# A bidirectional encoder layer on one core: row work between the layer's parts moved from GpSimd to VectorE, other tile order at the MLP's start, load order and held-back steps of the down products

## The chip, the core and the metric

One core of a Trainium2 chip. The time is the device time of one execution in microseconds (us); before is the median of three runs, beside one execution that was profiled. Engines are named as in the profile: PE (TensorE), ACT (ScalarE), DVE (VectorE), POOL (GpSimd), SP (SyncE, which issues the DMAs here).

## The reference, cut

```python
def trunk(x, ...):                       # x: prompt 256 tokens, sample 1024 tokens, D = 1024
    h = rms_norm(x, g_pre_mix)
    m = mixer(h, ...)                    # attention and retention branches, ends with merged @ w_out
    x = x + rms_norm(m, g_post_mix)
    h = rms_norm(x, g_pre_mlp)
    u = square(relu(h @ w_up))           # w_up 1024 x 4096
    return x + rms_norm(u @ w_down, g_post_mlp)   # w_down 4096 x 1024
```

Everything is float32. The prompt and the sample run through the same weights.

## The kernel before, in words

The 1280 tokens are ten row tiles of 128: tiles 0 and 1 are the prompt, 2 to 9 the sample. Each float32 product is made of three reduced-precision ones: `split` (L55) makes a high part on ACT (L57) and a low part on DVE (L58), and `mm3` (L60) issues high by high, high by low, low by high (L63 to L65). The kernel is written for a scheduler that orders each engine's instructions by a model of their times and by data dependences; pools of tiles add dependences when their space is used again.

**Seam 1**, at the end of `phase_merge`. `mm(t, u, w)` (L958) makes a quarter of w_out's product for row tile t in 24 matmuls of 256 columns, squares it on ACT with a running sum, and multiplies it by the gain on DVE (L965). `norm(t0)` (L967) does two row tiles: a reciprocal root on DVE (`rstd`, L67 to L80, 11 small instructions), the scaled add to x (for tiles 0 to 5 on ACT, L978, and POOL, L979; for tiles 6 to 9 one fused instruction on DVE, L975), a square sum on ACT (L981), a second root, and the scaling to the MLP's input (L985). `trow` (L996) transposes 128 x 512 of it on PE (four transposes, one bank) and splits the bank. The MLP's products are done by a scheme of seven products with sums and differences of blocks: the sums of row tiles (L1035, four for each of four pairs; those of i = 0 and 1 on POOL, those of 2 and 3 on DVE) are transposed into T[0] to T[2] and X[2] (from `tx` and from `mp`), the plain tiles into X[0] (prompt) and X[1]. The prompt's tiles come last in the w_out product, and its transposes last of all.

**The up phase** (`up(i)`, L1167, i = 0 to 15) runs seven products p1 to p7 and two plain ones for the prompt (c1, c2); `up_raw` loads the weights and `fprep` prepares their block sums (POOL) and splits. The results are squared and written to HBM as u rows (`u_s`, L1246).

**The down phase** (L1248 on) runs seven products over i = 0 to 15, in the order 1, 2, 6, 7, 4, 5, 3. `dprep(p, i)` loads a u row (`ur`, three buffers, L1264), in products 1 and 2 two weight tiles (`wd`, L1260), and splits both; `step` issues 15 matmuls for the five banks. `product(..., last)` holds the last steps back, so that each bank's matmuls of those steps come together. `part` squares half a row tile on ACT (L1319) and multiplies it by the gain on POOL (L1321); `final` has ten small DVE instructions and the scaled add of x (tiles 0 to 4: first half on ACT, L1340, and POOL, L1341, second half on DVE, L1343).

Of the kernel before, what the change touches and what calls it, by code (L numbers as in the profile page):

```python
# [35 lines left out]
FORD0 = ("A11", "A12", "S2", "S3", "S1", "A21", "A22", "S4")  # L36
# [12 lines left out]
class Build:  # L49
# [10 lines left out]
    def mm3(self, out, lhs, rhs, start, stop, more=False):  # L60
        (lh, ll), (rh, rl) = lhs, rhs
        mm = self.nc.tensor.matmul
        mm(out, lhsT=lh, rhs=rh, start=start, stop=False, skip_group_check=more)  # L63
        mm(out, lhsT=lh, rhs=rl, start=False, stop=False, skip_group_check=more)  # L64
        mm(out, lhsT=ll, rhs=rh, start=False, stop=stop, skip_group_check=more)  # L65
# [795 lines left out]
    def phase_merge(self):  # L861
# [105 lines left out]
        def norm(t0):  # L967
            ss = self.small.tile([P, 2], F32, tag="ss2", name="ss2")
            nc.vector.tensor_reduce(ss, ssa[:, t0:t0 + 2], AX.X, ALU.add)
            r = self.rstd(self.small, ss, D, 2)  # L970
            sx = self.small.tile([P, 2], F32, tag="sx2", name="sx2")
            for i in range(2):
                t = t0 + i
# [35 lines left out]
        for t in range(2, 6):  # L1009
            load_x(t)  # L1010
        self.up_raw(0)
        for t in range(2, 6):
            mm(t, 2, wo[2])
        self.fprep(0)
        self.fprep(1)
# [8 lines left out]
        for t in range(2, 6):  # L1024
            for h in range(2):
                trow(ms_[t][:, h * 512:(h + 1) * 512], X[1], 4 * h, (t - 2) * P)
        for u in (2, 3):
            for t in range(2):
                mm(t, u, wo[u])
        a_, b_ = slice(0, 512), slice(512, D)  # L1030
        t2s = []
        for i in range(4):
            xa, xb = ms_[2 + i], ms_[6 + i]
            e = nc.gpsimd if i < 2 else nc.vector
            sub = lambda o, x, y: e.tensor_tensor(o, x, y, ALU.subtract)  # L1035
            t2s.append(self.uw.tile([P, 512], F32, tag="t2", name="t2", bufs=3))
            sub(xa[:, a_], xb[:, a_], xa[:, a_])
            sub(t2s[i], xb[:, b_], xa[:, a_])
            sub(xb[:, a_], xb[:, b_], xb[:, a_])
            sub(xa[:, b_], xa[:, b_], t2s[i])  # L1040
        norm(0)
        self.close("mx", "w8r", "w8")
        tx = self.open("tx", 1)
        T = [(tx.tile([P, 4, 512], F32R, name=f"t{i}h"), tx.tile([P, 4, 512], F32R, name=f"t{i}l"))
             for i in range(3)]
        xtile(2)
        for j in range(5):
            for i in range(4):
                xa, xb = ms_[2 + i], ms_[6 + i]
                s, d, k = ((t2s[i], T[0], 0), (xb[:, a_], T[1], 0), (xa[:, a_], X[2], 0),  # L1050
                           (xa[:, b_], T[2], 0), (xb[:, b_], X[2], 4))[j]
                trow(s, d, k, i * P)
        for t in range(2):
            for h in range(2):
                trow(ms_[t][:, h * 512:(h + 1) * 512], X[0], 4 * h, t * P)
        self.X, self.T = X, T
        self.ul = self.open("ul", 1)
        self.sraw = [self.ul.tile([P, 4, P], F32, name=f"sr{i}") for i in range(4)]

    def up_raw(self, i):  # L1060
# [10 lines left out]

    def fprep(self, n):
# [7 lines left out]
        tt = nc.gpsimd.tensor_tensor  # L1080
        if f in ("A11", "A12", "A21", "A22"):
            src = {"A11": A11, "A12": A12, "A21": A21, "A22": A22}[f]
        else:
            s1, s2, s3, s4 = self.sraw
            if f == "S2":
                tt(s1, A21, A22, ALU.add)
                tt(s2, s1, A11, ALU.subtract)
            elif f == "S3":
                tt(s3, A11, A21, ALU.subtract)
            elif f == "S4":  # L1090
                tt(s4, A12, s2, ALU.subtract)
            src = {"S1": s1, "S2": s2, "S3": s3, "S4": s4}[f]
        if self.nfac % 6 < 3:
            p, tg = self.uw, "fe"
        else:
            p, tg = self.ul, "fl"
        self.nfac += 1
        hi = p.tile([P, 4, P], F32R, tag=tg + "h", name=tg + "h", bufs=3)
# [348 lines left out]
```

## Time and profile before

| | us |
|---|---|
| median of three runs (lowest, highest) | 2219.25 (2215.68, 2220.7) |
| the profiled execution's own time | 2216.62 |
| its span, first to last instruction | 2214.8 |
| PE busy in the span | 2078.1 (94%) |
| DVE busy | 1371.0 (62%) |
| ACT busy | 944.2 (43%) |
| POOL busy | 789.9 (36%) |

The profiled execution lies 1.8 us above its own span and 2.63 below the median. The up phase runs from about 1389 to 1790, the down phase from there to 2195.6, both with PE busy nearly all the time. What an engine waited for is read from rows that name the instruction that released it.

### The profile page before, as it was taken

To read this page: it belongs to the slowest core of one execution; us is meant where nothing else is said; L and a number is where in the kernel's file an instruction comes from. 1 tells how busy PE (TensorE), PEld (TensorE's weight loads), DVE (VectorE), ACT (ScalarE), POOL (GpSimd) and SP (SyncE) were. 2 spreads that over 40 slices of the span, in tenths; PEclk is the share of its full clock that TensorE was granted. 3 is DMA by queue.
4 is the path that set the end of the run, shared out by engine and by line. 5 is a ranking of instruction groups with operands and counts; after the bars stand their busy time and mean duration, and the time that the engine had idled before them with its cause. 6 is when DMAs were issued, how large, how long until landed. Compare 5 with 4: busy or idle time off the path is not lost. (4 is left out here: it accounts for less than half of the span.)

```text
span 2214.8 us, 32535 instructions
## 1 busy us (share of the span) xinstructions
PE 2078.1 (94%) x11856; PEld 1803.3 (81%) x11856; DVE 1371.0 (62%) x2754; ACT 944.2 (43%) x1912; POOL 789.9 (36%) x598
## 2 busy tenths in 40 slices
PE   7899999999988889898999995999999997999996
PEld 7788888888877778777888995888888875888885
DVE  7734645555599899987424429555555536754566
ACT  6422222222356666655423434444444433433442
POOL 1212111111056666665134524344444309720112
PEclk8999999999999999999999997999999999999998
DMA  3351111110322222221644512244333376333543
GB/s 146 120 187 39 43 41 41 41 41 25 104 58 83 71 84 84 75 64 58 221 161 131 167 48 105 86 141 148 135 123 128 136 272 235 99 100 96 164 139 113
DMA packets 169568, 241.09 MB, mean 109 GB/s; under 512 B 15768, under 2 KB 104768, under 8 KB 169408
## 3 DMA queue, kind: packets, MB, share of 16 engines
q1 hardware_dynamic: 161408, 230.82, 31.9%
q10 hardware_dynamic: 8000, 8.20, 1.1%
q8 instruction: 93, 1.52, 0.3%
q14 instruction: 67, 0.55, 0.1%
HBM read 159.91 MB, written 79.05 MB: 108 GB/s over the span
## 5 line engine op out<-in xcount | busy, mean ns | idle before, releaser
L63 PE MATMUL ps<-wh,uh 128*128 128x512 f32 x560 | 218.0, 395 | 17.2 <-ACT uh L57 12.2
L64 PE MATMUL ps<-wl,uh 128*128 128x512 f32 x560 | 219.9, 393 | 1.2 <-DVE wl L58 1.2
L65 PE MATMUL ps<-wh,ul 128*128 128x512 f32 x560 | 214.7, 390 | 0.0
L58 DVE TENSOR_TENSOR ul<-ur,uh 128x640 fp32r<-128x640 f32 x112 | 110.6, 990 | 144.4 <-ACT uh L57 144.4
L57 ACT CAST uh<-ur 128x640 fp32r<-128x640 f32 x112 | 81.8, 731 | 211.3 <-PE ps L64 177.5
L748 POOL TENSOR_TENSOR t<-s 128x1024 f32<-128x1024 f32 (+1 forms) x40 | 92.0, 2299 | 167.9 <-ACT s L742 109.9
L711 DVE TENSOR_REDUCE mx<-s 128x256 f32<-128x2048 f32 (+1 forms) x40 | 130.5, 3263 | 23.6 <-ACT s L706 23.4
L63 PE MATMUL ps<-hTh,wgh 128*128 128x512 f32 (+1 forms) x384 | 141.4, 368 | 2.4 <-ACT s L706 1.6
L63 PEld LDWEIGHTS ps<-wh,uh 128*128 128x128 f32 x560 | 106.5, 190 | 41.5 <-ACT uh L57 14.0
L64 PE MATMUL ps<-hTl,wgh 128*128 128x512 f32 (+1 forms) x384 | 138.3, 360 | 0.0
L65 PE MATMUL ps<-hTh,wgl 128*128 128x512 f32 (+1 forms) x384 | 138.3, 360 | 0.0
L63 PE MATMUL ps<-wah,hTh 128*128 128x512 f32 x320 | 127.9, 400 | 0.0
L64 PEld LDWEIGHTS ps<-wl,uh 128*128 128x128 f32 x560 | 106.4, 190 | 24.2 <-DVE wl L58 2.0
L65 PE MATMUL ps<-wah,hTl 128*128 128x512 f32 x320 | 125.0, 391 | 0.0
L64 PE MATMUL ps<-wal,hTh 128*128 128x512 f32 x320 | 124.7, 390 | 0.0
L65 PEld LDWEIGHTS ps<-wh,ul 128*128 128x128 f32 x560 | 105.7, 189 | 22.0
L58 POOL TENSOR_TENSOR el<-s,eh 128x1024 fp32r<-128x1024 f32 (+1 forms) x40 | 95.0, 2375 | 67.3 <-ACT eh L57 67.3
L507 POOL TENSOR_TENSOR qk<-t,t 128x256 f32<-128x256 f32 x40 | 29.4, 736 | 241.1 <-DVE t L503 194.0
L58 DVE TENSOR_TENSOR wl<-wd,wh 128x512 fp32r<-128x512 f32 x112 | 102.4, 914 | 20.5 <-ACT wh L57 20.5
L1177 POOL TENSOR_TENSOR a<-a 128x640 f32<-128x640 f32 x64 | 85.9, 1353 | 75.6 <-ACT a L1200 59.3
L500 DVE TENSOR_TENSOR t<-ps,rcs 128x256 f32<-128x256 f32 x40 | 17.0, 424 | 154.2 <-ACT v L494 136.8
L1321 POOL TENSOR_TENSOR acc<-acc,g 128x512 f32<-128x512 f32 x20 | 29.2, 1487 | 211.7 <-ACT jk L1319 211.7
(339 smaller groups left out, 6770.4 us busy)
## 6 DMA issues: line engine op xcount, KB each, us to landing
u_s<-a SPq DMA_DIRECT2D x112, 320.0 KB
ur<-u_s SPq DMA_DIRECT2D x112, 320.0 KB
uraw<-w_up SPq DMA_DIRECT2D x32, 512.0 KB
wd<-w_down SPq DMA_DIRECT2D x64, 256.0 KB
wraw<-w_in SPq DMA_DIRECT2D x24, 512.0 KB
x<-xs SPq DMA_DIRECT2D x16, 512.0 KB
g_s<-g SPq DMA_DIRECT2D x32, 256.0 KB
sg<-g_s SPq DMA_DIRECT2D x32, 256.0 KB
```

The costliest lines, as they stand in the source:

```text
L57: nc.scalar.copy(hi, src)
L58: (eng or nc.vector).tensor_tensor(lo, src, hi.bitcast(F32), ALU.subtract)
L63: mm(out, lhsT=lh, rhs=rh, start=start, stop=False, skip_group_check=more)
L64: mm(out, lhsT=lh, rhs=rl, start=False, stop=False, skip_group_check=more)
L65: mm(out, lhsT=ll, rhs=rh, start=False, stop=stop, skip_group_check=more)
L500: nc.vector.tensor_tensor(t0, pv, bc(rcs[:, pt, 0]), ALU.mult)
L507: nc.gpsimd.tensor_tensor(qk[:, 0:4].rearrange("p (j b) d -> p j b d", j=2), dup(t0[:, 0:2]), dup(t1[:, 0:2]), ALU.add)
L711: nc.vector.tensor_reduce(mx, s[:, 0:u[2]].rearrange("p k q -> p q k"), AX.X, ALU.max)
L748: nc.gpsimd.tensor_tensor(t[:, 0:n], src[:, 0:n], src[:, n:2 * n], ALU.add)
L1177: nc.gpsimd.tensor_tensor(r[:, s], r[:, s], r[:, s], ALU.mult)
L1321: nc.gpsimd.tensor_tensor(acc[t][:, c], acc[t][:, c], g3[:, c], ALU.mult)
```

## The change

It has four parts.

- **Norms and sums on DVE.** `norm` takes any row tiles and makes the scaled add of all of them with the fused DVE instruction; all the row sums are DVE's. The block sums of the first weights (`fsums`, on POOL) are made early, S3 and S4 in place.
- **Order at seam 1.** All row tiles but 7, 8, 9 get their third quarter first; norms go in the order 0/1, 2/3, 4/5, 6/7, 8, 9. The steps p1, p2, c1, c2 of `up(0)` come before the sums are transposed (`tprep`, called inside `up(0)`). T[0] and T[1] now lie in X[2], and T[2] to T[4] (T4, T1, B22) in `tx`.
- **Down loads.** In `dprep`, the two weight loads of products 1 and 2 are queued behind their own u row (`issue_after` adds an order on the issuing engine, no wait). In product 6 one block subtraction is made a product earlier.
- **The end.** Six steps of product 3 are held back instead of four, two of them in buffers of `wd`; `step` keeps the tiles in order; the gain of the last half row tiles and both halves of `final` are DVE's.

```diff
-        def norm(t0):
+        def norm(*ts):
+            t0, nt = ts[0], len(ts)
...
-                if t0 >= 6:
-                    nc.vector.scalar_tensor_tensor(xs[t], ms_[t], r[:, i:i + 1], xs[t], ALU.mult,
-                                                   ALU.add)
-                else:
-                    nc.scalar.activation(ms_[t], ms_[t], AF.Copy, scale=r[:, i:i + 1])
-                    nc.gpsimd.tensor_tensor(xs[t], xs[t], ms_[t], ALU.add)
+                nc.vector.scalar_tensor_tensor(xs[t], ms_[t], r[:, i:i + 1], xs[t], ALU.mult,
+                                               ALU.add)
...
-        for t0, t2 in ((2, (6, 7)), (4, (8,)), (6, (9,)), (8, ())):
+        for t0, t2 in ((0, 6), (2, 7), (4, 8)):
             for t in (t0, t0 + 1):
                 mm(t, 3, wo[3])
-            norm(t0)
-            for t in t2:
-                mm(t, 2, wo[2])
+            norm(t0, t0 + 1)
+            mm(t2, 2, wo[2])
         xtile(0)
         xtile(1)
...
+        nat(0, 1)
+        mm(6, 3, wo[3])
+        mm(7, 3, wo[3])
+        norm(6, 7)
+        mm(9, 2, wo[2])
+        nat(2, 3)
+        mm(8, 3, wo[3])
+        norm(8)
+        mm(9, 3, wo[3])
+        norm(9)
+        nat(4, 5)
...
-            e = nc.gpsimd if i < 2 else nc.vector
-            sub = lambda o, x, y: e.tensor_tensor(o, x, y, ALU.subtract)
...
+        def tprep():
+            sub = lambda o, x, y: nc.vector.tensor_tensor(o, x, y, ALU.subtract)
...
+            T = [(X[2][0][:, 0:4], X[2][1][:, 0:4]), (X[2][0][:, 4:8], X[2][1][:, 4:8])]
...
+            T += [(tx.tile([P, 4, 512], F32R, name=f"t{i}h"),
+                   tx.tile([P, 4, 512], F32R, name=f"t{i}l")) for i in range(3)]
...
+            if i == 0:
+                s_p1()
+                s_p2()
+                s_c1()
+                s_c2()
+                for n in range(4, 7):
+                    self.fprep(n)
+                self.tprep()
...
-                order = ((s_p1, 0), (s_p2, 1), (s_p6, 2), (s_p7, 3), (s_c1, 3), (s_p5, 4),
-                         (s_c2, 6), (s_p4, 6), (s_p3, 7))
+                order = ((s_p6, 4), (s_p7, 5), (s_p4, 6), (s_p5, 6), (s_p3, 7))
...
-        def dprep(p, i):
+        def dprep(p, i, wide=False):
             uraw = us.tile([P, HB], F32, tag="ur", name="ur", bufs=3)
-            nc.sync.dma_start(out=uraw, in_=self.u_s[UIDX[p], i])
-            for j, h in {1: ((0, 0), (1, 0)), 2: ((1, 1), (0, 1))}.get(p, ()):
-                load_wd(i, j, h)
+            ld = nc.sync.dma_start(out=uraw, in_=self.u_s[UIDX[p], i])
+            with self.tc.issue_after(ld.ins):
+                for j, h in {1: ((0, 0), (1, 0)), 2: ((1, 1), (0, 1))}.get(p, ()):
+                    load_wd(i, j, h)
...
+                with self.tc.issue_after(end.ins) if end and len(fs) > 1 else nullcontext():
+                    for n, (uh, ul, wh, wl) in enumerate(fs):
+                        end = self.mm3(bs[j], (uh[:, s], ul[:, s]), (wh, wl), start and n == 0,
+                                       stop and n == len(fs) - 1, more)
...
-            nc.gpsimd.tensor_tensor(acc[t][:, c], acc[t][:, c], g3[:, c], ALU.mult)
+            e = nc.vector if t < 5 and c is hi_ else nc.gpsimd
+            e.tensor_tensor(acc[t][:, c], acc[t][:, c], g3[:, c], ALU.mult)
...
-                if t < 5 and c is lo_:
-                    nc.scalar.activation(y, y, AF.Copy, scale=r)
-                    nc.gpsimd.tensor_tensor(y, y, x[:, c], ALU.add)
-                else:
-                    nc.vector.scalar_tensor_tensor(y, y, r, x[:, c], ALU.mult, ALU.add)
+                nc.vector.scalar_tensor_tensor(y, y, r, x[:, c], ALU.mult, ALU.add)
...
-        product(3, bc, False, 4)
-        for j in range(6):
-            if j < 5:
-                add(q1[j][:, hi_], q1[j][:, hi_], bc[j])
-                part(j, hi_)
-            if j:
-                final(j - 1)
+        product(3, bc, False, 6)
+        for j in range(5):
+            add(q1[j][:, hi_], q1[j][:, hi_], bc[j])
+            part(j, hi_)
+            final(j)
```

PE at the seam, before: `t_` are row sums (t2), `m_13099` and `m_13100` the rows of the sample, `m_13098` those of the prompt; `w8h` is w_out, `feh` the first up weight.

```order
L65 MATMUL ps<-w8h,mTl_12573 128x256
L999 MATMUL ps<-ident,t_14481 128x128 x4
L999 MATMUL ps<-ident,t_14486 128x128 x4
L999 MATMUL ps<-ident,t_14491 128x128 x4
L999 MATMUL ps<-ident,t_14496 128x128 x4
L999 MATMUL ps<-ident,m_13100 128x128 x16
L999 MATMUL ps<-ident,m_13099 128x128 x32
L999 MATMUL ps<-ident,m_13100 128x128 x16
L999 MATMUL ps<-ident,m_13098 128x128 x16
L63 MATMUL ps<-h2h_14315,feh 128x512
L64 MATMUL ps<-h2l_14316,feh 128x512
L65 MATMUL ps<-h2h_14315,fel 128x512
```

PE at the same place of the changed kernel; the first row is the last one of the steps p1, p2, c1, c2, and `h2h_14684` is X[2], that is T[0], with which p6 begins.

```order
L65 MATMUL ps<-h2h_14255,fel 128x512
L994 MATMUL ps<-ident,t_14686 128x128 x4
L994 MATMUL ps<-ident,m_13100 128x128 x4
L994 MATMUL ps<-ident,t_14705 128x128 x4
L994 MATMUL ps<-ident,m_13100 128x128 x4
L994 MATMUL ps<-ident,t_14724 128x128 x4
L994 MATMUL ps<-ident,t_14734 128x128 x4
L994 MATMUL ps<-ident,m_13100 128x128 x8
L994 MATMUL ps<-ident,m_13099 128x128 x32
L994 MATMUL ps<-ident,m_13100 128x128 x16
L63 MATMUL ps<-h2h_14684,feh 128x512
```

The transposes of the sums stood between the last w_out matmul and the first up matmul; they now stand behind four steps of the up phase, and the prompt's transposes are gone from here.

SP at the start of the down phase, before: `a` are the last up results, `ur` the u rows, `wd_` the down weights.

```order
L1246 DMA u_s<-a_14735 128x640
L1264 DMA ur<-u_s 128x640 x3
L1246 DMA u_s<-a_14733 128x640
L1264 DMA ur<-u_s 128x640
L1260 DMA wd_18122<-w_down 128x512
L1246 DMA u_s<-a_14733 128x640
L1260 DMA wd_18123<-w_down 128x512
L1260 DMA wd_18124<-w_down 128x512
L1260 DMA wd_18125<-w_down 128x512
L1260 DMA wd_18126<-w_down 128x512
```

SP at the same place of the changed kernel:

```order
L1405 DMA g_18619<-g_post_mlp 128x1024
L1291 DMA u_s<-a_14862 128x640
L1309 DMA ur<-u_s 128x640
L1305 DMA wd_18147<-w_down 128x512
L1291 DMA u_s<-a_14862 128x640
L1305 DMA wd_18148<-w_down 128x512
L1309 DMA ur<-u_s 128x640
L1305 DMA wd_18149<-w_down 128x512
L1305 DMA wd_18150<-w_down 128x512
L1309 DMA ur<-u_s 128x640
L1305 DMA wd_18151<-w_down 128x512
L1305 DMA wd_18152<-w_down 128x512
```

The weight loads stood in runs with four u rows ahead of them; now each u row is followed by its own two weight loads.

DVE in the last two tiles, before: `q_` are the small columns of `final`, `acc` the outputs, `x_` the rows that are added.

```order
L1343 SCALAR_TENSOR_TENSOR acc_18114<-acc_18114,q_21321,x_20772 128x512
L1336 SCALAR_TENSOR_TENSOR q_21341<-q_21341 128x1
L1327 SCALAR_TENSOR_TENSOR q_21357<-ssd 128x1
L1343 SCALAR_TENSOR_TENSOR acc_18114<-acc_18114,q_21341,x_20774 128x512
L1329 TENSOR_SCALAR q_21357<-q_21357 128x1
```

DVE at the same place of the changed kernel (`g_18619` is the gain):

```order
L1376 TENSOR_TENSOR acc_18139<-acc_18139,g_18619 128x512
L1382 SCALAR_TENSOR_TENSOR q_21376<-ssd 128x1
L1391 SCALAR_TENSOR_TENSOR q_21357<-q_21357 128x1
L1384 TENSOR_SCALAR q_21376<-q_21376 128x1
L1386 TENSOR_SCALAR q_21376<-q_21376 128x1
L1394 SCALAR_TENSOR_TENSOR acc_18139<-acc_18139,q_21357,x_20799 128x512 x2
L1387 TENSOR_SCALAR q_21376<-q_21376 128x1
```

Each tile has the gain and two final instructions on DVE, where it had one final instruction there.

## Rows read from the trace of the kernel before

**Rows 1.** the page: its first line and the share of the busiest engine (busy us, instructions).

```profile
span 2214.8 us, 32535 instructions
...
PE 2078.1 (94%) x11856; PEld 1803.3 (81%) x11856; DVE 1371.0 (62%) x2754; ACT 944.2 (43%) x1912; POOL 789.9 (36%) x598
```

**Rows 2.** TensorE's waits from 1295 to 1400: us in total, times, longest.

```profile
PE ps L999 <- DVE t L1035: 11.6, 1, 11.6
PE ps L999 <- POOL t L1035: 5.3, 2, 3.5
```

**Rows 3.** TensorE's waits from 1400 to the end.

```profile
PE ps L63 <- ACT uh L57: 12.2, 4, 6.3
PE ps L63 <- ACT wh L57: 5.0, 1, 5.0
PE ps L64 <- DVE wl L58: 1.2, 1, 1.2
```

**Rows 4.** windows: length, busy us of each engine, granted clock, DMA share, GB/s.

```profile
1349.05:1389.10 40.05, 17.62 (x98) 14.86 (x98) 38.31 (x75) 20.23 (x39) 22.03 (x14) 0.70 0.21 80
1800.00:1826.00 26.00, 26.00 (x116) 21.56 (x115) 10.11 (x15) 9.05 (x14) 0.00 (x0) 1.00 1.02 383
1826.00:1854.00 28.00, 15.75 (x52) 11.42 (x52) 7.72 (x8) 5.67 (x9) 23.76 (x18) 0.82 0.99 365
2195.70:2214.80 19.10, 0.00 (x0) 0.00 (x0) 14.50 (x41) 4.95 (x9) 9.15 (x7) 0.63 0.37 137
```

**Rows 5.** timeline of TensorE: start, us, engine, line, operation, count, [idle before, releaser].

```profile
1388.94 0.50 PE L63 MATMUL ps<-h2h,feh 128*128 128x512 f32 x1
...
1794.77 1.65 PE L63 MATMUL ps<-wh,uh 128*128 128x512 f32 x3 [4.98 <-ACT wh L57]
...
2195.25 0.39 PE L65 MATMUL ps<-wh,ul 128*128 128x512 f32 x1
```

**Rows 6.** timeline of VectorE at seam 1, and one row of the tail.

```profile
1334.38 2.48 DVE L975 SCALAR_TENSOR_TENSOR x<-m,rs_r,x 128x1024 f32<-128x1024 f32 x2
...
1337.17 4.26 DVE L58 TENSOR_TENSOR h2l<-ps,h2h 128x512 fp32r<-128x512 f32 x7
...
1346.86 4.52 DVE L975 SCALAR_TENSOR_TENSOR x<-m,rs_r,x 128x1024 f32<-128x1024 f32 x2
...
1357.45 1.25 DVE L78 SCALAR_TENSOR_TENSOR rs_t<-rs_t,rs_m 128x2 f32<-128x2 f32 x2
1358.67 0.23 DVE L79 SCALAR_TENSOR_TENSOR rs_r<-rs_t,rs_r 128x2 f32<-128x2 f32 x2
...
1360.04 1.42 DVE L985 TENSOR_SCALAR m<-x,rs_r 128x1024 f32<-128x1024 f32 x2
1361.37 3.43 DVE L1035 TENSOR_TENSOR m<-m,m 128x512 f32<-128x512 f32 x2
1364.72 2.83 DVE L1035 TENSOR_TENSOR t<-m,m 128x512 f32<-128x512 f32 x1
...
2196.86 1.25 DVE L1336 SCALAR_TENSOR_TENSOR q<-q 128x1 f32<-128x1 f32 x1
```

**Rows 7.** timeline of GpSimd at seam 1 and at the end.

```profile
1346.42 3.87 POOL L1035 TENSOR_TENSOR m<-m,m 128x512 f32<-128x512 f32 x2 [17.74 <-PE ps L65]
...
1361.34 5.67 POOL L979 TENSOR_TENSOR x<-x,m 128x1024 f32<-128x1024 f32 x2 [2.72 <-ACT m L978]
...
2210.64 1.26 POOL L1341 TENSOR_TENSOR acc<-acc,x 128x512 f32<-128x512 f32 x1 [2.98 <-ACT acc L1340]
```

**Rows 8.** timeline of ScalarE at seam 1 and at seam 2.

```profile
1349.20 1.06 ACT L981 ACTIVATE m<-x 128x1024 f32<-128x1024 f32 x1 [2.30 <-DVE x L975]
...
1788.51 2.32 ACT L57 CAST uh<-ur 128x640 fp32r<-128x640 f32 x3 [1.04 <-DMA ur<-u_s]
```

**Rows 9.** timeline of SyncE's DMA issues at seam 2.

```profile
1785.53 1.27 SPq L1264 DMA_DIRECT2D ur<-u_s  x3
...
1828.58 10.72 SPq L1260 DMA_DIRECT2D wd<-w_down  x16
```

More of the change, by code (lines that the diff above doesn't have):

```diff
@@ L1 @@
-from contextlib import ExitStack
+from contextlib import ExitStack, nullcontext
 import numpy as np
@@ L64, in mm3 @@
         mm(out, lhsT=lh, rhs=rl, start=False, stop=False, skip_group_check=more)
-        mm(out, lhsT=ll, rhs=rh, start=False, stop=stop, skip_group_check=more)
+        return mm(out, lhsT=ll, rhs=rh, start=False, stop=stop, skip_group_check=more)
     def rstd(self, pool, ss, n, width):
@@ L1008, in phase_merge, with nat @@
         wo[3] = wu(wvo, 3)
-        for t in range(2, 6):
+        for t in range(4):
             load_x(t)
+        self.sraw = [self.uw.tile([P, 4, P], F32, name=f"sr{i}") for i in range(2)]
         self.up_raw(0)
-        for t in range(2, 6):
+        def nat(*ts):
+            for t in ts:
+                x, o = (X[0], 0) if t < 2 else (X[1], 2)
+                for h in range(2):
+                    trow(ms_[t][:, h * 512:(h + 1) * 512], x, 4 * h, (t - o) * P)
+        for t in range(6):
@@ new lines, in phase_merge, with sums, tr @@
+        nat(4, 5)
+        a_, b_ = slice(0, 512), slice(512, D)
+        def tprep():
+            sub = lambda o, x, y: nc.vector.tensor_tensor(o, x, y, ALU.subtract)
+            t2s = {}
+            def sums(i, j):
+                xa, xb = ms_[2 + i], ms_[6 + i]
+                if j == 0:
+                    t2s[i] = self.uw.tile([P, 512], F32, tag="t2", name="t2", bufs=3)
+                    sub(xa[:, a_], xb[:, a_], xa[:, a_])
+                    sub(t2s[i], xb[:, b_], xa[:, a_])
+                elif j == 1:
+                    sub(xb[:, a_], xb[:, b_], xb[:, a_])
+                else:
+                    sub(xa[:, b_], xa[:, b_], t2s[i])
+            xtile(2)
+            T = [(X[2][0][:, 0:4], X[2][1][:, 0:4]), (X[2][0][:, 4:8], X[2][1][:, 4:8])]
+            def tr(i, j):
+                xa, xb = ms_[2 + i], ms_[6 + i]
+                s = (t2s.get(i), xb[:, a_], xa[:, b_], xa[:, a_], xb[:, b_])[j]
+                trow(s, T[j], 0, i * P)
+            for i in range(2):
+                for j in range(3):
+                    sums(i, j)
+                tr(i, 0)
+                tr(i, 1)
+            for i in (2, 3):
+                sums(i, 0)
+                tr(i, 0)
+            for i in (2, 3):
+                sums(i, 1)
+                tr(i, 1)
+            for i in (2, 3):
+                sums(i, 2)
+            self.close("mx", "w8r", "w8")
+            tx = self.open("tx", 1)
+            self.ul = self.open("ul", 1)
+            T += [(tx.tile([P, 4, 512], F32R, name=f"t{i}h"),
+                   tx.tile([P, 4, 512], F32R, name=f"t{i}l")) for i in range(3)]
+            for j in (2, 3, 4):
+                for i in range(4):
+                    tr(i, j)
+            self.T = T
@@ L1194, in s_p7 @@
                 prod(pb[0], i, "S3", "T3", False, True)
-                add(U3, V1, pb[0])
+                add(sums["U3"], V1, pb[0])
             def s_p4():
@@ L1204, in s_p5 @@
                 prod(pc[0], i, "S1", "T1", True, True)
-                add(r2[:, o2], U3, pc[0])
+                add(r2[:, o2], sums["U3"], pc[0])
                 nc.scalar.activation(r2[:, o2], r2[:, o2], AF.Relu)
@@ L1220, in s_c2 @@
                 conv(pv[1][:, 0:256], i, ("A21", "A22"))
+                if i:
+                    nc.scalar.activation(r2[:, 0:256], pv[1][:, 0:256], AF.Relu)
+            if i == 0:
[6 more added lines that the diff above has]
+                self.tprep()
+                T = self.T
+                xf.update(T2=(T[0], 0), T3=(T[1], 0), T4=(T[2], 0), T1=(T[3], 0), B22=(T[4], 0))
+                a1 = ac.tile([P, 4096], F32, tag="ac1", name="a1")
+                a2 = ac.tile([P, 4096], F32, tag="ac2", name="a2")
+                sums["U2"], sums["U3"] = a1[:, 0:512], a1[:, 512:1024]
+                US.extend(a1[:, 1024 + k * HB:1024 + (k + 1) * HB] for k in range(4))
+                rows.extend(a2[:, k * T_:(k + 1) * T_] for k in range(3))
+                r2 = rows[1]
                 nc.scalar.activation(r2[:, 0:256], pv[1][:, 0:256], AF.Relu)
```

136 lines of the change are left out of this document (54 added, 82 removed).

## The prediction

> **What bounds the kernel now.** I read the page's shares first: TensorE is busy for 2078.1 of 2214.8 us [rows 1], so a change to another engine pays only where TensorE stands still or runs at its lower clock. Then I asked for TensorE's waits stretch by stretch, and for windows around the longest. From the w_out product on there are three such places. **Seam 1** lies between w_out and the MLP: from the last w_out matmul at 1349.05 to the first up matmul at 1388.94 [rows 4, 5]. TensorE is busy there for 17.62 of 40.05 us, at a mean granted clock of 0.70, VectorE for 38.31: VectorE bounds that stretch. The long waits are for the seam's row sums, 11.6 us for VectorE's and 5.3 for GpSimd's [rows 2]. **Seam 2** is the start of the down products: 4.98 us ahead of the first down matmul [rows 5], then 12.2 us of waits for the cast of a reloaded u row, the longest 6.3, and 1.2 for a weight's low half [rows 3]. **The tail** runs from the last matmul (2195.25 + 0.39 = 2195.64) to the span's end at 2214.8: 19.15 us without a matmul [rows 4, 5]. In between, TensorE goes on without a listed wait, and the change leaves that work as it is: I cost it at nothing, with TensorE itself as the cover.
>
> **Seam 1, work added and relieved.** The norms of tiles 0 to 5 lose their scaling on ScalarE and their add on GpSimd, and get one fused VectorE instruction each, as tiles 6 to 9 had: 2.48 us for two [rows 6], 6 x 1.24 = 7.4. Eight sums move from GpSimd to VectorE at about 0.60 each (seven instructions of that size took 4.26 [rows 6]): 4.8. That is 12.2 us more, though most of the 7.4 now falls ahead of 1349, where TensorE covers it. Against it stands what GpSimd's work costs VectorE now. GpSimd is busy from 1346.42 and again from 1361.34 [rows 7]; beside it two fused instructions take 4.52 instead of 2.48, a pair of small ones 1.25 instead of 0.23, two sums 3.43 instead of 1.28 and one sum 2.83 instead of 0.68 [rows 6] (the last two clean values from 0.60 each and 0.08 for the end). The excess is 2.0, five small steps of 1.0 and 2 x 2.15: 11.3 us. With GpSimd out of the seam these should come clean, so added and relieved work nearly cancel, and the gain comes from what TensorE does meanwhile.
>
> **Seam 1, the order.** The prompt tiles are normalised first, so the last w_out products are those of tiles 8 and 9; behind them stand the transposes of tiles 4 and 5 and four steps of the first up group (24 matmuls of 512 columns and 48 of 256; 116 of 512 took 26.00 us [rows 4], 0.224 each, and half of it for the others: about 11.1 us). Call M the last w_out matmul, 1349.05, since TensorE has the same 40 products and 32 transposes ahead of it. VectorE then has this to do until the sums of the last tile, 9, are made, at the clean durations of [rows 6]: a backlog of 3.2; nine low halves of 0.60 (5.4); three chains of reciprocal roots, 11 steps each at 0.20 (6.6); four scalings of 0.67 and two fused instructions of 1.24 (5.2); fifteen sums of 0.60 (9.0); and 4 to 5 us of waiting for ScalarE's sums of squares (1.06 each [rows 8], with the way there and back) ahead of the chains of tiles 8 and 9. About 34. TensorE can't pass its eighty transposes before some fifteen more VectorE instructions have freed the banks, 9 to 10 us: the next up step, p6, starts at about M + 43.7 = 1392.7. The same point before is 1388.94 + 11.1 = 1400.0. Gain 7.5 us. Bounds: 13, if half the waiting overlaps and the evictions keep pace; 2, if only half of the 11.3 is relieved.
>
> **Seam 2.** Before, weight loads go out on SyncE's queue in runs, sixteen in 10.72 us at 1828.58 [rows 9], while the next u row's load stands behind them. Now each u row is followed by its own two weight loads. From the issue of the first u rows (1785.53 [rows 9]) to the cast of one (1788.51 [rows 8]) takes 3.0 us. The new first row has to wait for the very last up matmul, since T[4] now lives in the space that it takes. So the first wait doesn't vanish: 3.0, a cast of 0.6 and the weight's make 4.2 to 4.5 against 4.98. I keep also the 1.2 for the low half. What goes is the 12.2 [rows 3] and the lower clock that came with those waits: between 1826 and 1854 the clock was 0.82, and 52 matmuls were busy for 15.75 us [rows 4] where 52 x 0.224 = 11.7 would do; some records may be missing, and I take 3.1 of these 4. A product step of 15 matmuls is 3.4 us and needs one u row (0.33 MB) and two weights (0.52 MB): 250 GB/s, where 365 were moved in that stretch [rows 4], so loads stay ahead. Gain 12.2 + 3.1 + 0.5 = 15.8; bounds 11 (a third of the later waits stays) and 18 (the low half's goes too).
>
> **Tail.** Six steps instead of four are held back, so the last tiles come 18 matmuls (4.1 us) apart instead of 12 (2.7), and VectorE's work for one tile fits between: an add and the gain 0.60 each, ten steps of the root 2.1, two fused instructions of 0.67: 4.6, of which the steps of two tiles overlap. Then only the last tile stands behind the last matmul: add 0.7, square on ScalarE 0.8 (an estimate from 1.06 for twice the width), gain 0.6, steps 2.1, two fused 1.4, and 1.6 for the tile before and for handing over: 7.2. After GpSimd's last instruction (2210.64 + 1.26 = 2211.90 [rows 7]) the end came 2.9 us later; 7.2 + 2.9 = 10.1 against 19.15. Gain 9; bounds 6 (VectorE a tile behind) and 11. That ScalarE and GpSimd lose two steps per tile costs nothing: VectorE's are shorter, and GpSimd's delay it (1.25 for a single small step beside them [rows 6]).
>
> **Sum.** 7.5 + 15.8 + 9 = 32.3 us off the profiled 2216.62: 2184.3. The median of the three runs shown is 2219.25, 2.63 above that; 2219.25 - 32.3 = 2187.
>
> **Rivals.** (1) Seam 1 is bound by VectorE, and the change gives it more. If its slow rows come from its own chains and not from GpSimd, the 11.3 us don't come back: p6 starts at M + 55, and seam 1 loses 4 instead of winning 7.5: 2198. For it: 38.31 of 40.05 us busy [rows 4]. Against it: the pair of small instructions is back at 0.23 at 1358.67, when GpSimd's first stretch is over [rows 6]. Chance 0.17. The Trainium skill (Perfetto Trace Analysis, Optimizing Scalar/DVE Operations) says that work may be taken off a saturated VectorE, to GpSimd if need be, which speaks against this change; the same paragraph warns that the two share a read port, so that moving work between them may not help. The trace bears the second half out with 0.23 against 1.25; by the first half alone the time would be this rival's 2198.
>
> (2) Part of the later waits at the down start stays, since the paced loads all start behind the last up matmul, and three u buffers bound how far the rows run ahead: seam 2 wins 5 instead of 15.8: 2198. For it: the first u rows went out at 1785.53 [rows 9], four us ahead of the last up matmul, and now go out behind it. Against: 250 of 365 GB/s. Chance 0.10.
>
> (3) The tail doesn't do what it should: VectorE, which takes over the last steps, trails TensorE, and the last chain is as long as now: no gain of 9, 2196. Against: 4.6 us without overlap against 4.1 per tile, so five tiles trail by 2.5 us at most. Chance 0.07.
>
> (4) Slower: pacing makes each of the 32 steps of products 1 and 2 wait for its own round trip. It decides if a u row isn't issued before the step ahead of it has ended: a step is then 3.0 + 0.7 + 0.6 = 4.3 to 4.4 instead of 3.4 us, and at the clock of 0.82 that such waits gave [rows 4] its matmuls take 0.75 more: 32 x 1.75 = 56 us in place of the 15.3 removed, 2219.25 - 32.3 + 56 = 2243. Against: there are three u buffers, and three rows went out together before [rows 9]. Chance 0.04.
>
> **How the numbers follow.** The forecast has a chance of 0.62: the bounds of its terms add up to gains of 19 at the least and 42 at the most, 2177 to 2200 with 2187 near the middle. Rivals (1) to (3) end at 2196 to 2198 one by one and near 2207 two together; (4) lies outside. The range, 2176 to 2203, leaves out (4), the pairs and the forecast's edges. About 0.2% (4.4 us) is what a measurement of this kernel can tell from no change. Below 2214.8 lie all cases but (4) and the few in which three terms fail together: faster 0.93, within 0.2% 0.03, slower 0.04.
>
> **What would show it.** Seam 1: the first up matmul 5 to 8 us behind the last w_out matmul, four steps at the full clock, then transposes that wait for VectorE, no GpSimd rows, small pairs at 0.23 throughout, and p6 near 1392. If pairs stay at 1.25, rival (1). Seam 2: one first wait of 4 to 5 us, and then no wait for a u cast over 1 us. Waits of about 1 us at every step mean (4), a few long ones (2). Tail: about 10 us between the last matmul and the end, the last five tiles 4.1 us apart. The forecast is wrong if TensorE's waits from the first down matmul on sum to over 10 us, or if p6 starts after 1397.

## The result, and the profile after

| | before | changed |
|---|---|---|
| median, us (four executions each) | 2218.57 | 2189.77 |
| lowest to highest | 2215.68 to 2220.7 | 2184.92 to 2191.16 |
| profiled execution's span | 2214.8 | 2188.9 |

The ratio is 0.9867, 95% interval 0.9848 to 0.9887: 25 to 34 us faster, 28.8 by the medians. 2187 was forecast. The spans differ by 25.9 only, and the missing part lies ahead of the change: the first w_out matmul started at 1233.29 in the trace of before and at 1237.30 in that of after, with the same work ahead of it. Over all traces of this study it lies between 1232.8 and 1237.3, and the last w_out matmul ends between 1349.1 and 1354.0. I therefore count from that end: 865.8 us to the span's end before, 836.8 after, 29.0 less. The w_out stage itself, from its first matmul to its last, took 114.8 to 119.0 us in the kernels whose row work is moved and 115.8 to 119.0 in those of before's program, so the moved work shows no price there.

TensorE's waits in the changed kernel, first from 1290 to 1400 and then from 1400 to the end (us in total, times, longest), to be held against [rows 2, 3]:

```profile
PE ps L994 <- DVE t L1041: 15.6, 2, 9.9
PE ps L63 <- ACT h2h L57: 1.4, 1, 1.4
...
PE ps L63 <- ACT wh L57: 5.8, 1, 5.8
PE ps L63 <- DVE acc L1191: 2.6, 1, 2.6
```

The waits for u rows, 12.2 us in [rows 3], are gone. The wait ahead of the first down matmul is longer, 5.8, and one for `acc` is new. Seam 1 still waits for VectorE's sums, now 15.6 us. The timeline of TensorE shows the places at which these waits end, the start of p6 (1394.82) and the last matmul, as in [rows 5]:

```profile
1355.25 0.62 PE L63 MATMUL ps<-h2h,feh 128*128 128x512 f32 x2 [1.38 <-ACT h2h L57]
...
1394.82 0.50 PE L63 MATMUL ps<-h2h,feh 128*128 128x512 f32 x1
...
1790.68 2.50 PE L63 MATMUL ps<-wh,uh 128*128 128x512 f32 x5 [5.83 <-ACT wh L57]
...
1959.63 0.47 PE L63 MATMUL ps<-wh,uh 128*128 128x512 f32 x1 [2.58 <-DVE acc L1191]
...
2178.73 0.39 PE L65 MATMUL ps<-wh,ul 128*128 128x512 f32 x1
```

From the last matmul (2179.12) to the end at 2188.9 it is 9.8 us, 19.2 before. The windows from the end of w_out to p6 in the changed kernel, and to the first up matmul in a variant told of below, *steps_not_ahead*, stand against the first line of [rows 4]:

```profile
1352.20:1394.80 42.60, 25.59 (x168) 23.08 (x166) 39.80 (x110) 22.77 (x48) 5.74 (x4) 0.80 0.30 107
...
1353.00:1391.90 38.90, 15.44 (x97) 14.56 (x95) 35.66 (x106) 17.91 (x37) 0.00 (x0) 0.65 0.26 95
```

VectorE is busy in 39.80 of 42.60 us, so it bounds the seam as before. TensorE has 25.59 us of work there instead of 17.62, and GpSimd 5.74 instead of 22.03.

All kernels of this study, cut at the same places of their traces. "Seam 1" runs from the end of w_out to p6, or to the first up matmul (marked *) where the four steps are not ahead; "up" from there to the end of the last up matmul; "wait" to the first down matmul; "down" from that to the end of the last matmul; "tail" to the span's end; "all" is the sum, taken before rounding.

| kernel | seam 1 | up | wait | down | tail | all |
|---|---|---|---|---|---|---|
| before | 39.9* | 400.9 | 5.0 | 400.9 | 19.2 | 865.8 |
| changed | 42.7 | 390.0 | 5.8 | 388.4 | 9.8 | 836.8 |
| steps_not_ahead | 38.9* | 401.3 | 6.0 | 388.2 | 9.7 | 844.1 |
| sums_on_gpsimd | 46.6 | 390.1 | 6.4 | 388.5 | 9.8 | 841.3 |
| norms_on_gpsimd | 46.3 | 390.1 | 6.2 | 388.1 | 9.8 | 840.4 |
| no_pacing | 42.8 | 390.0 | 5.6 | 402.3 | 9.7 | 850.4 |
| pacing_alone (on before) | 40.7* | 400.9 | 4.9 | 387.0 | 19.2 | 852.6 |
| gain_load_later | 42.9 | 390.0 | 4.7 | 388.6 | 9.8 | 836.0 |
| sums_not_ahead | 42.9 | 390.1 | 6.3 | 384.1 | 9.8 | 833.1 |
| four_held_back | 42.8 | 390.0 | 6.2 | 388.2 | 11.9 | 839.2 |
| tail_on_gpsimd | 43.0 | 390.0 | 6.1 | 387.8 | 11.5 | 838.4 |
| tile_order_free | 42.9 | 390.0 | 5.8 | 388.3 | 10.1 | 837.2 |
| tile_order_alone (on before) | 39.9* | 400.9 | 5.0 | 399.3 | 14.8 | 859.8 |
| both_fixed | 42.2 | 390.0 | 3.5 | 382.4 | 9.8 | 828.0 |

Stages that an edit does not touch agree within 0.8 us, except the down stage with before's loads (400.9 and 399.3, where the tile order of the last steps differs too). The wait is 5.8 to 6.4 in the eight kernels with the same loads at that place, and seam 1 of before's program 39.9 to 40.7. A median with an interval is given for kernels that were run four or five times; the others were run once, and of them only the stages are compared.

### The profile page after: what moved, and what is told of

It is laid out like the page before. It is cut to its first block, busy times and chain, and to the rows that moved or that the text cites. A ratio compares the mean times of both kernels' runs of the same rounds, so it can differ in the third digit from the quotient of the medians.

```text
span 2188.9 us, 32539 instructions
## 1 busy us (share of the span) xinstructions
PE 2075.1 (95%) x11856; PEld 1802.5 (82%) x11856; DVE 1407.4 (64%) x2803; ACT 933.1 (43%) x1901; POOL 759.7 (35%) x574
## 4 chain that ended last, share of the span: by engine, by line
PE 73%; DVE 10%; issue 6%; ACT 4%; DMA 4%; POOL 3%; SPq 0%; DVEq 0%; ACTq 0%; POOLq 0%
PE ps L63 22%; PE ps L65 22%; PE ps L64 22%; POOL t L748 2%; ACT s L706 1%; DVE el L58 1%; PE ps L540 1%; PE ps L543 1%; DVE s L740 1%; DVE mx L711 1%; ACT s L742 1%; PE ps L521 1%; PE ps L586 1%; PE ps L585 1%; DVE ql L58 1%
## 5 line engine op out<-in xcount | busy, mean ns | idle before, releaser
L63 PE MATMUL ps<-wh,uh 128*128 128x512 f32 x550 | 209.3, 393 | 8.4 <-ACT wh L57 5.8
L58 DVE TENSOR_TENSOR ul<-ur,uh 128x640 fp32r<-128x640 f32 x110 | 123.8, 1125 | 114.4 <-ACT uh L57 114.3
L63 PE MATMUL ps<-h2h,feh 128*128 128x512 f32 (+1 forms) x352 | 117.8, 337 | 1.4 <-ACT h2h L57 1.4
L64 PE MATMUL ps<-h2l,feh 128*128 128x512 f32 (+1 forms) x352 | 118.5, 337 | 0.0
L65 PE MATMUL ps<-h2h,fel 128*128 128x512 f32 (+1 forms) x352 | 118.1, 337 | 0.0
```

The lines of the kernel that those rows point to most:

```text
L58: (eng or nc.vector).tensor_tensor(lo, src, hi.bitcast(F32), ALU.subtract)
L65: return mm(out, lhsT=ll, rhs=rh, start=False, stop=stop, skip_group_check=more)
```

## Experiments at seam 1

**steps_not_ahead.** The four steps go back behind the transposes of the sums:

```diff
-                s_p1()
-                s_p2()
-                s_c1()
-                s_c2()
                 for n in range(4, 7):
                     self.fprep(n)
                 self.tprep()
+                s_p1()
+                s_p2()
+                s_c1()
+                s_c2()
```

> The changed kernel with the four steps p1, p2, c1, c2 of the first up group behind the transposes of the row sums, as in the kernel before, instead of ahead of them. Theory (the gain at seam 1 is work laid under VectorE's chain): the transposes wait for VectorE as long as before, and the four steps' 11 us come behind: from the first w_out matmul to the first matmul of p6 157.5 us become 166 to 169, the time is 8 to 11 us above the changed kernel, 2198 to 2201. Rival (the gain is GpSimd's relief of VectorE, and the order is worth little): 158 to 161 us, 2190 to 2193.

Measured: 2196.2 us, ratio to before 0.9898 (0.9877 to 0.9919). Seam 1 and up together are 440.2 us against 432.7 of the changed kernel and 440.8 of before. (From the first w_out matmul to p6 it is 168.4 us, inside the 166 to 169 expected. But the w_out stage alone varies by 4 us, so I compare from its end; the whole, 844.1 against 836.8, is 7.3 more, a little less than the 8 to 11 expected.) So 7.5 of the 8.1 us that seam 1 wins go with the order, in which TensorE does four steps while VectorE works. What is left without that order, the moved row work and the other order of the row tiles, is worth 0.6, within the 0.8 by which seam 1 of before's program varies: the added and the relieved VectorE time nearly cancel.

**sums_on_gpsimd** and **norms_on_gpsimd.** Is the relief real, or would VectorE be better off without the work? The first edit gives the sums of two pairs of row tiles back to GpSimd, the second the scaled add of tiles 0 to 5 to ScalarE and GpSimd (both cut to the added lines).

```diff
+                e = nc.gpsimd if i < 2 else nc.vector
+                sub = lambda o, x, y: e.tensor_tensor(o, x, y, ALU.subtract)
```

```diff
+                if t < 6:
+                    nc.scalar.activation(ms_[t], ms_[t], AF.Copy, scale=r[:, i:i + 1])
+                    nc.gpsimd.tensor_tensor(xs[t], xs[t], ms_[t], ALU.add)
+                else:
```

> The changed kernel with the sums of the first two pairs of row tiles on GpSimd again, as in the kernel before; the rest of the change stays. Measured from the end of the last w_out matmul to the first matmul of p6, 42.7 us in the changed kernel. Theory (GpSimd's work beside VectorE slows it more than it takes from it): 44 to 49 us, with pairs of small VectorE instructions at 1.1 to 1.3 us while GpSimd runs. Rival (VectorE's own work bounds the seam, and 8 sums of 0.60 are taken from it): 37 to 41 us.

> The changed kernel with the scaled add of row tiles 0 to 5 on ScalarE and GpSimd again, as in the kernel before; the rest of the change stays. Theory: this work lies ahead of the last w_out matmul, where TensorE has its own work, so it costs little there, but the chain of tiles 4 and 5 gets longer and their transposes, which stand ahead of the pulled steps, wait for it: from the end of the last w_out matmul to p6 43 to 48 us instead of 42.7. Rival (VectorE is relieved of 7.4 us): 36 to 41 us.

Measured: 46.6 and 46.3 us, as the theories had it, 3.9 and 3.6 more than 42.7. In *sums_on_gpsimd* VectorE is busy for longer with fewer instructions, 43.68 us with 102 where the changed kernel has 39.80 with 110:

```profile
1354.00:1400.60 46.60, 26.46 (x168) 23.56 (x166) 43.68 (x102) 22.87 (x48) 18.69 (x12) 0.78 0.27 98
```

The timeline of VectorE in that kernel shows why, and below it that of GpSimd at the same time:

```profile
1366.67 1.78 DVE L58 TENSOR_TENSOR fel<-uraw,feh 128x512 fp32r<-128x512 f32 x1
...
1374.53 1.26 DVE L79 SCALAR_TENSOR_TENSOR rs_r<-rs_t,rs_r 128x1 f32<-128x1 f32 x2
1375.75 0.23 DVE L77 TENSOR_TENSOR rs_t<-rs_r 128x1 f32<-128x1 f32 x2
```

```profile
1374.43 1.26 POOL L1046 TENSOR_TENSOR m<-m,t 128x512 f32<-128x512 f32 x1
```

A low half with both operands in SBUF takes 1.78 us beside GpSimd's work, 0.69 in the changed kernel. A pair of one-column instructions takes 1.26 us, just as long as GpSimd's instruction beside it, and 0.23 right behind its end. An instruction with one operand in PSUM is not slowed: in the changed kernel three `h2l<-ps,h2h` took 0.62 each, from 1369.87 on, while GpSimd worked from 1370.82 to 1372.08:

```profile
1369.87 1.87 DVE L58 TENSOR_TENSOR h2l<-ps,h2h 128x512 fp32r<-128x512 f32 x3
```

```profile
1370.82 1.26 POOL L1103 TENSOR_TENSOR sr<-uraw 128x512 f32<-128x512 f32 x1 [1.42 <-ACT uraw L1094]
```

The Trainium skill (SBUF — State Buffer, SBUF: two separate sides) says that a VectorE instruction with two SBUF inputs and a GpSimd one that reads SBUF take a shared pair of ports as an exclusive lock: whichever starts first holds it, and the other waits for the whole instruction. The rows agree: 1.26 for 0.23, and no slowing with a PSUM operand.

In *norms_on_gpsimd* the cause is another, the one expected: GpSimd's adds end ahead of the last w_out matmul, but the rows of tiles 4 and 5 come later. TensorE waits for them behind w_out, which it does not do in the changed kernel:

```profile
PE ps L998 <- DVE m L984: 2.2, 1, 2.2
```

The wait for VectorE's sums is 1.1 us longer as well. So with the four steps ahead, taking back either part of the moved row work costs 3.6 to 3.9 us, while without them the whole move is worth 0.6: the gains of the order and of the row work do not simply add. What the order gives with both parts taken back was not run.

## Experiments at the down products

**no_pacing** and **pacing_alone** take the pacing out of the changed kernel, and put it alone into the kernel before:

```diff
-            with self.tc.issue_after(ld.ins):
+            with nullcontext():
```

```diff
-            nc.sync.dma_start(out=uraw, in_=self.u_s[UIDX[p], i])
-            for j, h in ...
-                load_wd(i, j, h)
+            ld = nc.sync.dma_start(out=uraw, in_=self.u_s[UIDX[p], i])
+            with self.tc.issue_after(ld.ins):
+                for j, h in ...
+                    load_wd(i, j, h)
```

> The changed kernel without the order that queues the two weight loads of a step behind its own u row; everything else of the change stays. SyncE's first thirteen or so issues at the start of the down phase are the same, then weight loads go in runs of 6 to 13 again. Theory (the pacing takes away the later waits for u rows): TensorE's waits for the cast of a u row come back in product 1, 9 to 13 us, with 2 to 4 us of lower clock, and the first wait stays at 5.5 to 6; the time is 11 to 16 us above the changed kernel, about 2201 to 2206, ratio to the kernel before about 0.993. Rival (the other layout of the sums, which lets u rows start later, already takes the runs apart): waits below 3 us, 2190.

> The kernel before with nothing but the pacing of the weight loads. Theory: the waits of 12.2 and 1.2 us go, and the lower clock with them; the first wait stays near 5, since the first weight's load still starts just behind the last up matmul. From the first down matmul to the last matmul 400.9 us become 386 to 389; the time is 12 to 15 us below before, 2204 to 2207. Rival (each step waits for its own round trip): about 1 us at each of 32 steps, 2230 or more. If a new wait of 2 to 3 us at the end of product 6 is due to denser work on GpSimd and VectorE, it is here too; if it is due to the block subtraction made a product earlier, it is not.

Measured: 2204.08 us, ratio 0.9933 (0.9914 to 0.9952), and 2207.2 us, 0.9948 (0.9929 to 0.9968). The down stage loses 13.9 us without the pacing and wins 13.9 with it alone (that the two are equal is chance, see the 1.6 us above): the later layout of the sums has no visible part in it. TensorE's waits, first *no_pacing*, then *pacing_alone*:

```profile
PE ps L63 <- ACT uh L57: 13.8, 5, 4.8
PE ps L63 <- ACT wh L57: 5.6, 1, 5.6
```

```profile
PE ps L63 <- ACT wh L57: 4.9, 1, 4.9
PE ps L63 <- DVE acc L1165: 2.5, 1, 2.5
```

The second also brings the wait for `acc`, with the block subtraction still in its old place; so that move isn't its cause. *no_pacing*, with the waits for u rows back, does not have it.

**sums_not_ahead.** Product 4's block difference goes into a pair of rotating buffers:

```diff
             elif p == 4:
-                tt(B21, B21, B11, ALU.subtract)
-                src = B21
+                src = fxp[0].tile([P, 512], F32, tag="jk", name="jk")
+                tt(src, B21, B11, ALU.subtract)
```

> The changed kernel with the block differences of product 4 written to a rotating pair of buffers instead of in place, so that GpSimd can make only two of them ahead and not all sixteen during product 6. Theory (the wait of 2.5 us at the end of product 6 is VectorE's queue, slowed beside GpSimd's unbroken work: u and weight low halves at 1.91 and 1.78 us make 3.5 us a step against 3.4 of TensorE): the wait goes, and from the first to the last down matmul 388.4 us become 385.5 to 386.5. Rival (the wait comes from the place of the five additions in VectorE's order, whatever GpSimd does): 2 us or more stay.

Measured: the list of TensorE's waits from 1785 on has one entry left, the first wait, and the stage takes 384.1 us, 4.4 less where 2 to 3 were expected:

```profile
PE ps L63 <- ACT wh L57: 6.3, 1, 6.3
```

The reason shows in the changed kernel's VectorE and GpSimd at the end of product 6:

```profile
1951.50 1.78 DVE L58 TENSOR_TENSOR wl<-wd,wh 128x512 fp32r<-128x512 f32 x1
1953.20 1.91 DVE L58 TENSOR_TENSOR ul<-ur,uh 128x640 fp32r<-128x640 f32 x1
1955.03 1.78 DVE L58 TENSOR_TENSOR wl<-wd,wh 128x512 fp32r<-128x512 f32 x1
1956.74 0.81 DVE L58 TENSOR_TENSOR ul<-ur,uh 128x640 fp32r<-128x640 f32 x1
```

```profile
1935.02 21.25 POOL L1324 TENSOR_TENSOR wd<-wd,wd 128x512 f32<-128x512 f32 x12
```

A step's two low halves take 1.83 + 1.70 = 3.5 us from start to start, more than TensorE's 3.4; VectorE falls behind, and the additions that free product 6's banks come late. Windows from 1900 to 1950, the changed kernel and *sums_not_ahead* (VectorE's and GpSimd's busy time are the third and fifth):

```profile
1900.00:1950.00 50.00, 50.00 (x222) 41.42 (x221) 50.00 (x30) 23.11 (x44) 50.00 (x29) 1.00 0.31 94
```

```profile
1900.00:1950.00 50.00, 50.00 (x223) 41.39 (x222) 27.78 (x30) 24.03 (x45) 14.69 (x9) 1.00 0.33 96
```

Of the 4.4 us, 2.6 are the wait. The other 1.8 fit the granted clock, which was 0.73 in the 6.4 us behind this wait in the changed kernel (6.4 x 0.27 = 1.7; the row stands in the last section).

**gain_load_later.**

```diff
-            ld = nc.sync.dma_start(out=uraw, in_=self.u_s[UIDX[p], i])
+            ld = self.ld = nc.sync.dma_start(out=uraw, in_=self.u_s[UIDX[p], i])
...
-        nc.sync.dma_start(out=g3, ...)
+        with self.tc.issue_after(self.ld.ins):
+            nc.sync.dma_start(out=g3, ...)
```

> The changed kernel with the load of the last gain (one 128 x 1024 tile from a broadcast row, 0.5 MB written) queued behind the u rows of the first down product instead of ahead of the first. The first down matmul came 5.83 us after the last up matmul, where 4.2 to 4.5 were expected: the u row took 4.5 us from issue to cast and the weight 4.7. Theory A (the gain's load, issued 2.8 us ahead of the u row, shares the DMA engines with it): the first wait becomes 4.3 to 4.9. Theory B (u row, weights and the stores of the last u rows get in each other's way, since the first u row now starts after the last up matmul): it stays at 5.4 to 6.2.

Measured: the first wait is 4.65 us, theory A, below all eight kernels with the load ahead (5.8 to 6.4):

```profile
1789.10 2.50 PE L63 MATMUL ps<-wh,uh 128*128 128x512 f32 x5 [4.65 <-ACT wh L57]
```

In the changed kernel the gain's load had moved to 1782.13, ahead of the first u row, as SyncE's and ScalarE's timelines show:

```profile
1782.13 0.33 SPq L1405 DMA_DIRECT2D g<-g_post_mlp  x1
1783.30 0.32 SPq L1291 DMA_DIRECT2D u_s<-a  x1
1784.88 0.32 SPq L1309 DMA_DIRECT2D ur<-u_s  x1
```

```profile
1789.39 0.72 ACT L57 CAST uh<-ur 128x640 fp32r<-128x640 f32 x1 [3.15 <-DMA ur<-u_s]
```

Issue to cast took 4.5 us, where [rows 8, 9] had 3.0 and *gain_load_later* 3.15 (1784.48 to 1787.63).

**both_fixed** has the last two edits, and two more: B22 goes to X[2] and T3 to `tx`, and each u row is queued behind the weights of the step before.

```diff
-                s = (t2s.get(i), xb[:, a_], xa[:, b_], xa[:, a_], xb[:, b_])[j]
+                s = (t2s.get(i), xb[:, b_], xa[:, b_], xa[:, a_], xb[:, a_])[j]
...
-            for j in (2, 3, 4):
+            for j in (4, 2, 3):
...
+            with self.tc.issue_after(self.lw.ins) if p in (1, 2) and i else nullcontext():
```

> The changed kernel with four repairs at the down phase: the gain's load behind the first product's u rows; the block B22 in X[2] and T3 in the space that the u rows take, so that the first u row needn't wait for the last up matmul; each u row queued behind the weights of the step before it; and the two-ahead buffers for product 4. Theory: the first wait is then the first weight's round trip alone, 4.0 to 4.5 us instead of 5.8, and the wait of 2.5 us is gone: 4 to 5 us less than the changed kernel, about 2185, ratio to the kernel before 0.984 to 0.986. Rival (the weight's load gets slower as the u row's did): first wait 5 to 6, 2187.

Measured: 2181.08 us, ratio to before 0.9828 (0.9813 to 0.9843), 8.7 us below the changed kernel by the medians and 8.8 from the end of w_out on, where 4 to 5 were expected: the fastest of this study, with an interval wholly below the changed kernel's (0.9848 to 0.9887). The u row is loaded ahead (1778.87), the first weight takes 2.8 us from 1783.17 to its cast, and the first wait is 3.5 instead of the 4.0 to 4.5 expected:

```profile
PE ps L63 <- ACT wh L57: 4.2, 3, 3.5
```

The down stage is 6.0 us shorter, which is more than the 2.6 of the wait. The clock accounts for the rest, as far as an estimate goes: 1.7 behind that wait, and behind the first one 1.00 instead of 0.55 over 6.4 us, 2.9, less 0.6 for two small new waits.

## Experiments at the tail

```diff
-        product(3, bc, False, 6)
+        product(3, bc, False, 4)
```

> The changed kernel with four steps held back in the last product instead of six. Theory: TensorE then ends a row tile every 2.7 us, VectorE needs 4.1 for one, so it falls behind by 1.4 us for each of four tiles: 9.8 us from the last matmul to the end become 14 to 16, everything else the same. Rival (the tail's gain comes from the work's move from GpSimd and ScalarE to VectorE alone): 9.5 to 11.

Measured: 11.9 us, between the two expectations. The theory's price was wrong: the additions of the first three tiles follow TensorE at 2.75 us,

```profile
2168.38 0.69 DVE L1191 TENSOR_TENSOR acc<-acc,ps 128x512 f32<-128x512 f32 x1 [0.83 <-PE ps L65]
...
2171.13 0.69 DVE L1191 TENSOR_TENSOR acc<-acc,ps 128x512 f32<-128x512 f32 x1
...
2173.85 0.69 DVE L1191 TENSOR_TENSOR acc<-acc,ps 128x512 f32<-128x512 f32 x1
```

and only the last two fall behind, 2.8 and 3.7 us apart (2176.66, 2180.39). So the 4.1 us that VectorE spends on a tile hold waiting that it fills when tiles come faster, and 2.1 us are lost, not 4 to 6.

In **tail_on_gpsimd** the gain, and the scaled add of half of each row tile, are as before:

```diff
-            e = nc.vector if t < 5 and c is hi_ else nc.gpsimd
-            e.tensor_tensor(acc[t][:, c], acc[t][:, c], g3[:, c], ALU.mult)
+            nc.gpsimd.tensor_tensor(acc[t][:, c], acc[t][:, c], g3[:, c], ALU.mult)
...
+                if t < 5 and c is lo_:
+                    nc.scalar.activation(y, y, AF.Copy, scale=r)
+                    nc.gpsimd.tensor_tensor(y, y, x[:, c], ALU.add)
```

> The changed kernel with the gain of the last half row tiles on GpSimd and half of the last scaled adds on ScalarE and GpSimd again, as in the kernel before; six steps held back and the tile order stay. From the last matmul to the end 9.8 us in the changed kernel, 11.9 with four steps held back, 19.2 before. Theory (the move to VectorE carries most of the tail's gain, since GpSimd's instructions of 1.25 slow VectorE's beside them and lie in the last tile's chain): 13 to 17 us. Rival (the longer distance between tiles carries it): 10 to 12 us.

Measured: 11.5 us, the rival's range. That left the tile order. **tile_order_free** takes it out of the changed kernel, **tile_order_alone** puts it alone into the kernel before:

```diff
-                with self.tc.issue_after(end.ins) if end and len(fs) > 1 else nullcontext():
+                with nullcontext():
```

> The changed kernel without the fixed tile order in the held-back steps: the scheduler may mix the tiles' matmuls again. Theory (the order carries the tail): from the last matmul to the end 12 to 16 us instead of 9.8. Rival: 9.5 to 11.

> The kernel before with nothing but the fixed tile order in the held-back steps: four steps held back, and the last work on ScalarE, GpSimd and VectorE as before. Four held-back steps instead of six cost the changed kernel 2.1 us at the end, the last work on GpSimd 1.7, where the whole tail won 9.4. Theory (the order of the tiles carries the tail: before, three row tiles ended together 6 us ahead of the end and two at the end): from the last matmul to the end 19.2 us become 13 to 15.5. Rival (the parts need each other; the order alone brings little): 17 to 19.

Measured: 10.1 us without it, and 14.8 with it alone in before. Both readings were half right. In the kernel before, three tiles' additions came in one go (first line, VectorE); with the order alone all five come one by one (two of them shown):

```profile
2189.10 1.88 DVE L1165 TENSOR_TENSOR acc<-acc,ps 128x512 f32<-128x512 f32 x3 [5.06 <-PE ps L65]
```

```profile
2188.07 0.69 DVE L1165 TENSOR_TENSOR acc<-acc,ps 128x512 f32<-128x512 f32 x1 [0.82 <-PE ps L65]
...
2191.01 0.68 DVE L1165 TENSOR_TENSOR acc<-acc,ps 128x512 f32<-128x512 f32 x1
```

In the changed kernel they come 4.1 us apart, as forecast, the last right behind the last matmul (2179.12):

```profile
2175.08 0.69 DVE L1191 TENSOR_TENSOR acc<-acc,ps 128x512 f32<-128x512 f32 x1 [0.20 <-PE ps L65]
...
2179.20 0.68 DVE L1191 TENSOR_TENSOR acc<-acc,ps 128x512 f32<-128x512 f32 x1
```

The order alone wins 4.3 of the 9.4 us. Taking out any one of the three parts costs 0.3 (order), 1.7 (engine) or 2.1 (six steps), 4.1 together: the parts stand in for each other. How the remaining 5 us divide between two parts without the third was not run.

## Why the prediction was right, and where it was off

The sum was forecast at 32.3 us; from the end of w_out it is 29.0, and by the medians 28.8. The time lies 2.8 us above 2187, inside the range. That the time comes so close is in part luck: seam 2 brought 4.2 us less than forecast, seam 1 and the tail made up for 1.0 of them, and the median of before, of four runs now, is 0.7 lower than the one in the sum.

- **Seam 1**: 7.5 forecast, 39.9 + 400.9 less 42.7 + 390.0 = 8.1 measured. p6 starts 42.7 us behind the end of w_out, forecast 43.7. *steps_not_ahead* bears out both halves of the argument, that row work and relief cancel (0.6) and that the order gives the rest; but the two are not a sum, since with the order the row work is worth more (3.6 and 3.9 for its two parts). Rival (1) falls with p6 at 42.7 instead of 55, and with *sums_on_gpsimd*. Two signs named for this seam did not come: the first up matmul stands 3.1 us behind the last w_out matmul, not 5 to 8, and GpSimd still has four instructions there (5.74 us). The advice of the Trainium skill (Perfetto Trace Analysis, Optimizing Scalar/DVE Operations) to take work off a saturated VectorE doesn't hold towards GpSimd here, 46.6 against 42.7; the paragraph's own warning does.
- **Seam 2 is the term that was mis-sized**: 15.8 forecast, 11.6 measured (5.0 + 400.9 less 5.8 + 388.4), inside its bounds of 11 to 18. That the 12.2 us go was right, and that the pacing does it. Three things were missed. The first wait grew by 0.85 instead of shrinking by 0.5: the prediction lets the u row take the 3.0 us of before's row and does not price the gain's load, though the order of the changed kernel shows it right ahead; with it moved the wait is 4.65, near the forecast of 4.2 to 4.5. The clock behind that wait was 0.55 and not 0.76 as in before. And around the removed waits GpSimd had worked while VectorE had little to do (23.76 and 7.72 of 28 us [rows 4]): without them its sums lie beside VectorE's low halves throughout, and a wait of 2.6 us appears at the end of product 6, with 1.7 more in clock. The prediction put that stretch at nothing, covered by TensorE, without asking whether VectorE keeps pace there. On the other side the 1.2 for the low half, which it kept, went too, and the clock of the removed waits gave back some 4 to 5 us instead of 3.1 (an estimate: the 13.9 us of *pacing_alone*, less 13.4 of waits, plus 2.5 for the new wait and about 1.5 for its clock).
- **Tail**: 9 forecast, 9.4 measured, 9.8 us where 10.1 was worked out. But the reason given, the distance of 4.1 us between tiles against VectorE's 4.6, was only one of three that can replace each other.
- Rival (4) did not come: no step of products 1 and 2 waits for its u row. The remaining rivals (2) and (3) are excluded by the stage times.
- The start of w_out differs by up to 4.5 us and its end by 4.9 between traces, and no step of the prediction covers that; it is more than half of the term for seam 1.

## What to carry to other kernels

Read a wait that is removed as time that other engines used: ask which pair of engines loses its gap, and whether the slower of them still keeps pace with the step. When a bound engine can't be relieved, lay independent work of the waiting engine under its chain; that was worth 7.5 us here. The move of the row work was worth next to nothing without that order, but with it each part that was taken back cost 3.6 to 3.9 us, so try such parts together as well as one by one. Where several loads share a queue, check in the issue order what stands ahead of the first one that somebody waits for, since half a megabyte there cost 1.2 us.

## What the runs showed of the hardware

The granted clock behind a wait does not follow the wait's length alone. Windows of 6.4 us from the first down matmul, in the kernel before (wait 4.98), the changed kernel (5.83), *gain_load_later* (4.65) and *both_fixed* (3.52); the third figure from the end is the clock, 1.00 being the 2.4 GHz level and 0.50 the 1.2 GHz one:

```profile
1794.80:1801.20 6.40, 6.40 (x22) 5.17 (x23) 4.88 (x7) 1.84 (x3) 0.00 (x0) 0.76 0.96 326
```

```profile
1790.70:1797.10 6.40, 6.40 (x16) 4.67 (x17) 6.40 (x10) 2.60 (x4) 0.00 (x0) 0.55 1.03 399
```

```profile
1789.10:1795.50 6.40, 6.40 (x21) 4.92 (x22) 5.92 (x10) 2.58 (x4) 0.00 (x0) 0.74 1.01 355
```

```profile
1786.70:1793.10 6.40, 6.02 (x25) 4.49 (x26) 5.00 (x7) 2.04 (x4) 0.00 (x0) 1.00 0.92 292
```

After 3.52 us nothing was lost, in this one trace; after 2.58 us at the end of product 6 the changed kernel ran at 0.73:

```profile
1959.60:1966.00 6.40, 6.37 (x21) 5.11 (x22) 4.21 (x7) 0.00 (x0) 0.00 (x0) 0.73 0.33 109
```

The same wait, 2.4 to 2.7 us, stands in nine traces; the clock behind it was 0.73 in seven of them, 0.76 in *pacing_alone* and 0.52 in *gain_load_later*. So a short wait in the middle of full work cost 2.6 us and 1.7 us more in clock, while a longer one elsewhere cost only itself. What decides it was not tried.
